# MLP up projection by seven block products instead of eight, with the down projection woven between them

## The chip, the cores and the metric

The kernel runs on one core of one Trainium2 chip. The core has a matrix engine (TensorE, PE in the profile; its weight loads are PEld), three engines for elementwise work (VectorE or DVE, ScalarE or ACT, GpSimd or POOL), a fifth that issues most of the transfers (SyncE or SP), and 16 DMA engines between the main memory and the core's own memory. Matrix products land in PSUM, which has eight banks of 128 x 512 fp32 values. The metric is the device time of one execution in microseconds.

## The reference

A decoder trunk of two layers for 512 tokens of width 1024, in fp32. Each layer has a mixer (pooling and convolution in the first, latent attention in the second), cross-attention into 256 memory tokens, and the gated MLP that this change is about:

```python
def conv_ffn(h, w_up, conv_w, conv_b, w_down):
    a, g = jnp.split(h @ w_up, 2, axis=-1)
    g = causal_dwconv(g, conv_w) + conv_b
    return (jax.nn.silu(g) * a) @ w_down

x = x + conv_ffn(rmsnorm(x, norm_ffn_g[l]), ffn_w_up[l], ffn_conv_w[l], ffn_conv_b[l], ffn_w_down[l])
```

The inner width is 2816, which is 22 tiles of 128. `h @ w_up` has 2 x 22 tiles of output (a and g) and contracts over 1024, 8 tiles of 128; `w_down` contracts over 2816.

## The kernel before

Channels lie on the partitions and the 512 tokens along the free axis, so a tile of activations is 128 x 512. x, the residual stream, stays on chip as 8 such tiles.

Every product is made of three. A value is split into a high part (rounded to the fp32r type, by an ACT copy) and a low part (the value less the high part, by a DVE subtraction), and `mm3` (L156 to L159) adds high x high, high x low and low x high into one PSUM bank. A matmul has a 128 x 128 block of weights as its stationary operand and up to 512 tokens as the moving one. `load_w` (L147) loads 1024 columns of raw weights through SP (`load_raw`, L142, four buffers), casts the high part on ACT (L152) and subtracts the low part on DVE (L153), into three buffers each. These two steps are given a priority that is 40 places higher (`AHEAD`). `linear` (L183) is one output tile: load_w and then 3 matmuls for each k tile.

The order of the instructions on each engine is a planner's: it takes the program's order as priority, and takes a later instruction first where the earlier one isn't ready by its own estimate. Buffers come from pools: `slot` gives one of 58 tiles of 128 x 512 (`SLOTS`), `bank` one of the 8 PSUM banks.

The MLP is `ffn` (L466). Its input is x times the norm's gain, unscaled by the token's rate: the rate is known later (`norm.rate`, `norm.wide`), and is spread to a tile rb that each product is multiplied with on its way out of PSUM (L479, L490). `up(i)` handles a pair of tiles: the gate tile `KF + i`, its convolution over three tokens (ACT L485, DVE L486 and L487), silu (L488), then the tile i, their product (L491), and its split (`split_sb`, L193) into the list prod. After the 9th pair the down projection runs over the first 8 tiles of prod, after the 17th over the next 8, and over the last 6 at the end (`FFN_GROUPS`); each adds its 8 output tiles to x (L514), the last one in layer 0 through `residual` (L288), which also forms the next norm's input. In layer 1 the last group goes through `finale` (L517), which runs 256 tokens at a time. After the third pair of layer 0, `extra` makes the rotary tables (L838), some 20 DVE steps that the second layer's attention uses.

Keys and values of the memory tokens for layer 1 are computed in layer 0's mixer and kept in eight tiles of their own (`keep_whole`, L365) until `split_kv` (L370) at the end of the second layer's attention (L1075).

Of the kernel before, what the change touches and what calls it, by code (L numbers as in the profile page):

```python
# [11 lines left out]
F32 = mybir.dt.float32  # L12
# [7 lines left out]
P = 128  # L20
T = 512
# [29 lines left out]
SLOTS = 58  # L51
# [11 lines left out]
FFN_GROUPS = (8, 8, 6)  # L63

# columns of the packed per-channel constants
# [16 lines left out]
def _split_2pi():  # L82
    """2*pi*512 and 2*pi cut into parts whose products with the counts below are exact in float32."""
# [17 lines left out]
def kernel(ctx: ExitStack, tc: tile.TileContext, a):  # L101
# [7 lines left out]
    pp = ctx.enter_context(tc.tile_pool(name="pp", bufs=8, space=PSUM))  # L109

# [36 lines left out]
    def load_w(src, n):  # L147
        raw = load_raw(src, n)
        hi = wp.tile([P, WCOLS], F32R, tag="wh", name=uid("wh"), bufs=3)
        lo = wp.tile([P, WCOLS], F32R, tag="wl", name=uid("wl"), bufs=3)  # L150
        with tc.high_priority(offset=AHEAD):
            act.copy(hi[:, :n], raw[:, :n])  # L152
            vec.tensor_tensor(lo[:, :n], raw[:, :n], f(hi[:, :n]), ALU.subtract)  # L153
        return hi, lo

    def mm3(ps, ah, al, bh, bl, first, last):  # L156
        pe.matmul(ps, ah, bh, start=first, stop=False)  # L157
        pe.matmul(ps, ah, bl, start=False, stop=False)  # L158
        pe.matmul(ps, al, bh, start=False, stop=last)  # L159

    class Linear:
        """psum[m, t] = sum over k tiles of src[p, k * 128 + m] * xs[k][p, t], a range of k at a time."""

        def __init__(self, src, nk, ps=None):
            self.src, self.nk, self.w = src, nk, {}
            self.ps = bank("lin") if ps is None else ps

        def load(self, k):
            c = k // KD
            if c not in self.w:  # L170
                n = min(KD, self.nk - c * KD) * P
                self.w[c] = load_w(self.src[:, c * KD * P:c * KD * P + n], n)
# [10 lines left out]
    def linear(src, xs):  # L183
        return Linear(src, len(xs)).run(xs, 0, len(xs))
# [15 lines left out]
    def newton_rsqrt(v, n, name):  # L200
        """1/sqrt(v) of a narrow tile."""
# [13 lines left out]
    def col_sums(acc, n=TB):  # L215
        """sums over the partitions of acc, tokens on partitions: [128, n]."""
# [7 lines left out]
    def row_rate(src, n, name):  # L224
        """1/rms of tokens whose features lie along the free axis: [128, n]"""
# [16 lines left out]
    def spread(r, n=TB, name="rb", out=None):  # L242
        """[128, n] with tokens on partitions -> [128, n * 128] with tokens along the free axis."""
# [948 lines left out]
```

## Time and profile before

| | |
|---|---|
| runs | 1388.37 us median of 3 (1388.16 to 1388.73) |
| span of the profiled execution | 1386.6 us |
| what lies around it in the median | 1.8 us |
| first MLP, whole products | about 350 to 668 us |
| second MLP up to its finale | about 1025 to 1341 us |
| loads of weights for up and down in the MLPs | 88 and 48 |

The span is that of one profiled execution, from its first to its last instruction; the runs' median is 1.8 us longer. All times within the kernel below are from that execution, in us from the start of the span. A group's row of the profile gives line, engine, operation, tiles and shapes, a count, and then busy time and mean ns of one. In the timeline a row is start, duration, engine, line and operation. Durations of neighbours overlap on PE, and by somewhat less than 0.1 us on DVE and ACT, so that what an instruction costs its engine is read from the distance between starts.

### The profile page before, as it was taken

The numbers are of one execution on the slowest core, as the hardware profiler recorded it, in microseconds if no ns is written. First come the engines' busy times: TensorE is split into PE (matmuls) and PEld (weight loads), VectorE is DVE, ScalarE is ACT, GpSimd is POOL, SyncE is SP. The second block draws the span as 40 slices with busy tenths as digits, with TensorE's granted clock in tenths as the row PEclk, the third lists the DMA queues.
The fourth block names the chain that finished last, engine by engine and source line by source line (L and its number), as shares of the span: only waits on it lengthen the run. The fifth ranks groups of instructions, "written<-read, shape, count | busy, mean of one in ns | idle before, by whom it ended". The sixth has DMA issues, their size and how long they took to land.

```text
span 1386.6 us, 16884 instructions
## 1 busy us (share of the span) xinstructions
PE 1371.6 (99%) x6532; PEld 1131.2 (82%) x6532; DVE 889.0 (64%) x1535; ACT 599.2 (43%) x976; POOL 6.3 (0%) x17
## 2 busy tenths in 40 slices
PE   8999999999999999999999999999999999999997
PEld 6888978888888888888887776888888888888887
DVE  6999988555685366445669775755566544653565
ACT  6416456443443143223447786644443322332343
POOL 0000000000000000000100000000000000000000
PEclk9999999999999999999999999999999999999999
DMA  9235524113333333333321111321223333233221
GB/s 331 93 106 188 169 91 145 61 56 98 108 97 91 105 93 93 104 91 87 97 83 50 43 46 46 107 76 61 76 91 96 102 92 106 91 93 106 84 84 62
DMA packets 42560, 135.28 MB, mean 98 GB/s; under 512 B 4848, under 2 KB 6512, under 8 KB 42480
## 3 DMA queue, kind: packets, MB, share of 16 engines
q1 hardware_dynamic: 41904, 133.45, 31.0%
q8 instruction: 51, 0.84, 0.2%
q10 hardware_dynamic: 576, 0.76, 0.2%
q14 instruction: 29, 0.24, 0.1%
HBM read 132.09 MB, written 2.10 MB: 97 GB/s over the span
## 4 chain that ended last, share of the span: by engine, by line
PE 90%; DVE 7%; ACT 2%; issue 1%; DMA 0%; SPq 0%; DVEq 0%; ACTq 0%
PE lin L159 24%; PE lin L157 24%; PE lin L158 24%; DVE cv L677 3%; PE s L1016 1%; PE mpv L1053 1%; DVE wl L153 1%; PE t L1041 1%; PE vx L158 1%; PE vx L159 1%; PE fin L157 1%; PE vx L157 1%; PE fin L158 1%; PE fin L159 1%; ACT p L1024 1%
## 5 line engine op out<-in xcount | busy, mean ns | idle before, releaser
L152 ACT CAST wh<-wr 128x1024 fp32r<-128x1024 f32 (+3 forms) x240 | 239.0, 998 | 485.0 <-PE lin L158 338.4
L157 PE MATMUL lin<-hh,wh 128*128 128x512 f32 x976 | 382.4, 392 | 5.9 <-ACT hh L264 5.9
L158 PE MATMUL lin<-hl,wh 128*128 128x512 f32 x976 | 381.1, 391 | 0.0
L159 PE MATMUL lin<-hh,wl 128*128 128x512 f32 x976 | 380.8, 390 | 0.2 <-DVE wl L153 0.2
L153 DVE TENSOR_TENSOR wl<-wr,wh 128x1024 fp32r<-128x1024 f32 (+3 forms) x240 | 276.9, 1155 | 60.4 <-ACT wh L152 58.9
L157 PEld LDWEIGHTS lin<-hh,wh 128*128 128x128 f32 x976 | 183.8, 188 | 43.2 <-ACT hh L264 5.9
L158 PEld LDWEIGHTS lin<-hl,wh 128*128 128x128 f32 x976 | 183.7, 188 | 39.4 <-DVE hl L265 2.1
L159 PEld LDWEIGHTS lin<-hh,wl 128*128 128x128 f32 x976 | 183.7, 188 | 38.7 <-DVE wl L153 0.7
L158 PE MATMUL lin<-fl,wh 128*128 128x512 f32 x304 | 118.4, 389 | 0.0
L159 PE MATMUL lin<-fh,wl 128*128 128x512 f32 x304 | 118.3, 389 | 0.0
L157 PE MATMUL lin<-fh,wh 128*128 128x512 f32 x304 | 118.1, 389 | 0.0
L514 DVE TENSOR_TENSOR x<-x,lin 128x512 f32<-128x512 f32 x32 | 22.0, 688 | 102.8 <-PE lin L159 102.8
L479 DVE TENSOR_TENSOR g<-lin,rb 128x512 f32<-128x512 f32 x44 | 30.4, 690 | 79.2 <-PE lin L159 79.2
L677 DVE SCALAR_TENSOR_TENSOR cv<-a,con,cv 128x509 f32<-128x509 f32 (+25 forms) x115 | 79.5, 728 | 0.1
L490 DVE TENSOR_TENSOR g<-lin,rb 128x512 f32<-128x512 f32 x44 | 30.4, 691 | 71.6 <-PE lin L159 71.4
L158 PEld LDWEIGHTS lin<-fl,wh 128*128 128x128 f32 x304 | 57.1, 188 | 12.1 <-DVE fl L197 0.2
L157 PEld LDWEIGHTS lin<-fh,wh 128*128 128x128 f32 x304 | 57.1, 188 | 11.8
L159 PEld LDWEIGHTS lin<-fh,wl 128*128 128x128 f32 x304 | 57.1, 188 | 11.7
L488 ACT ACTIVATE c<-c 128x512 f32<-128x512 f32 x44 | 27.8, 633 | 82.1 <-DVE c L487 82.1
L289 DVE TENSOR_TENSOR x<-x,lin 128x512 f32<-128x512 f32 x40 | 27.3, 686 | 35.6 <-PE lin L159 35.6
L158 PE MATMUL lin<-ol,wh 128*128 128x512 f32 x128 | 50.1, 391 | 0.0
L159 PE MATMUL lin<-oh,wl 128*128 128x512 f32 x128 | 49.9, 390 | 0.0
(351 smaller groups left out, 2062.4 us busy)
## 6 DMA issues: line engine op xcount, KB each, us to landing
wr<-in_ffn_up SPq DMA_DIRECT2D x88, 512.0 KB, 3.5
wr<-in_ffn_down SPq DMA_DIRECT2D x32, 512.0 KB, 3.5
wr<-in_xa_wk SPq DMA_DIRECT2D x16, 512.0 KB, 3.7
wr<-in_xa_wv SPq DMA_DIRECT2D x16, 512.0 KB, 4.2
wr<-in_xa_wq SPq DMA_DIRECT2D x16, 512.0 KB, 3.6
wr<-in_xa_wo SPq DMA_DIRECT2D x16, 512.0 KB, 3.5
wr<-in_ffn_down SPq DMA_DIRECT2D x16, 384.0 KB, 3.1
wr<-in_pc_in SPq DMA_DIRECT2D x11, 512.0 KB, 6.6
```

The costliest lines, as they stand in the source:

```text
L152: act.copy(hi[:, :n], raw[:, :n])
L153: vec.tensor_tensor(lo[:, :n], raw[:, :n], f(hi[:, :n]), ALU.subtract)
L157: pe.matmul(ps, ah, bh, start=first, stop=False)
L158: pe.matmul(ps, ah, bl, start=False, stop=False)
L159: pe.matmul(ps, al, bh, start=False, stop=last)
L289: vec.tensor_tensor(x[m], x[m], ps, ALU.add)
L479: vec.tensor_tensor(g, gps, rb, ALU.mult)
L488: act.activation(c, c, AF.Silu)
L490: vec.tensor_tensor(g, aps, rb, ALU.mult)
L514: vec.tensor_tensor(x[m], x[m], ps, ALU.add)
L677: vec.scalar_tensor_tensor(cv[i][:, s:], gl[i][:, :T - s], w, cv[i][:, s:], ALU.mult, ALU.add)
L1016: pe.matmul(ps[i], q[:, i * P:(i + 1) * P], k[:, :P * (i + 1)], start=True, stop=True)
```

## The change

The first four pairs of each layer (`PLAIN_PAIRS`) are computed as before, apart from their weights' low parts. For the other 18, the pair's weights are seen as a 2 x 2 block matrix (rows: gate tile and up tile; columns: the two halves of the contraction) and the input as a 2 x 2 block matrix (the two halves of the contraction; the two halves of the tokens). Their product is formed by Winograd's variant of Strassen's scheme: seven block products instead of eight, each over 4 k tiles and 256 tokens, with three matmuls for each k tile as before. Three of the four PSUM groups go on to accumulate after they have been read in between. The operand on the input's side must hold sums of its blocks; `Operands.fill` forms them once a layer, in 32 steps, five after each product of plain pairs 1 to 3, from x scaled by gain and rate. The weights' sums are formed per pair by `Weights.piece`, on DVE.

For the plain pairs from the second on, and for the gate weights of every paired tile, the low part is made by ACT (minus the raw weights, rounded) and an accumulating DMA of POOL that adds the raw weights from main memory.

The down projection runs in groups of four k tiles and one of six. A step of it, three matmuls of 512 columns, follows each of the seven block products. The rotary tables are made after the last of these steps. High and low weights have four buffers instead of three, there are 59 slots, and layer 1's keys and values are stored to main memory and loaded again, instead of in eight tiles of their own.

The core of the diff (comments and docstrings that fall away are left out):

```diff
-SLOTS = 58
+SLOTS = 59
...
-FFN_GROUPS = (8, 8, 6)
+FFN_GROUPS = (4, 4, 4, 4, 6)
+PLAIN_PAIRS = 4
+OPERAND_STEPS = 5
+LEAD = 2
+HALF = T // 2
+KH = KD // 2
...
+    def parts():
+        hi = wp.tile([P, WCOLS], F32R, tag="wh", name=uid("wh"), bufs=4)
+        lo = wp.tile([P, WCOLS], F32R, tag="wl", name=uid("wl"), bufs=4)
+        return hi, lo
+    def low_by_dma(lo, raw, src):
+        act.mul(lo, raw, -1.0)
+        pool.dma_start(lo, src, accum_op=ALU.add)
+    def load_w(src, n, dma=False):
         raw = load_raw(src, n)
-        hi = wp.tile([P, WCOLS], F32R, tag="wh", name=uid("wh"), bufs=3)
-        lo = wp.tile([P, WCOLS], F32R, tag="wl", name=uid("wl"), bufs=3)
+        hi, lo = parts()
         with tc.high_priority(offset=AHEAD):
             act.copy(hi[:, :n], raw[:, :n])
-            vec.tensor_tensor(lo[:, :n], raw[:, :n], f(hi[:, :n]), ALU.subtract)
+            if dma:
+                low_by_dma(lo[:, :n], raw[:, :n], src)
+            else:
+                vec.tensor_tensor(lo[:, :n], raw[:, :n], f(hi[:, :n]), ALU.subtract)
...
     def keep_whole(ps, shape):
-        t = sl.tile(list(shape), F32, tag="kv1", name=uid("kv1"), bufs=8)
+        t = slot("kv1", F32, shape)
         act.copy(t, ps)
+        d = dr.tile(list(shape), F32, tag=uid("kv"), name=uid("kv"))
+        act.dma_start(d, t)
+        return d, shape
...
+    class Operands:
+        def fill(self):
+            low = None
+            for k in range(KH):
+                u = []
+                for kk in (k, k + KH):
+                    t = slot("u")
+                    vec.scalar_tensor_tensor(t, x[kk], col(self.norm.gain, self.norm.base + kk), self.rb,
+                                             ALU.mult, ALU.mult)
+                    u.append(t)
+                    yield
+                b11, b12 = u[0][:, :HALF], u[0][:, HALF:]
+                b21, b22 = u[1][:, :HALF], u[1][:, HALF:]
+                if k % 2 == 0:
+                    low = slot("bh", F32R), slot("bl", F32R)
+                c = slice(k % 2 * HALF, (k % 2 + 1) * HALF)
+                act.copy(low[0][:, c], b11)
+                vec.tensor_tensor(low[1][:, c], b11, f(low[0][:, c]), ALU.subtract)
+                self.v["b11"].append((low[0][:, c], low[1][:, c]))
+                yield
+                a, b = slot("ta"), slot("tb")
+                nt1, nt2 = a[:, :HALF], a[:, HALF:]
+                t3, t4 = b[:, :HALF], b[:, HALF:]
+                vec.tensor_tensor(nt1, b11, b12, ALU.subtract)
+                vec.tensor_tensor(t3, b22, b12, ALU.subtract)
+                yield
+                vec.scalar_tensor_tensor(nt2, t3, -1.0, b11, ALU.mult, ALU.subtract)
+                vec.scalar_tensor_tensor(t4, nt2, -1.0, b21, ALU.mult, ALU.subtract)
+                yield
+                for src, n0, n1 in ((a, "nt1", "nt2"), (u[1], "b21", "b22"), (b, "t3", "t4")):
+                    h, l = split_sb(src, "t")
+                    self.v[n0].append((h[:, :HALF], l[:, :HALF]))
+                    self.v[n1].append((h[:, HALF:], l[:, HALF:]))
+                    yield
+    class Weights:
...
+        def piece(self, n):
+            if n == 0:
+                self.g = load_raw(self.src[0], D)
+                self.r = load_raw(self.src[1], D)
+                hi, lo = parts()
+                act.copy(hi, self.g)
+                low_by_dma(lo, self.g, self.src[0])
+                self.put(("a11", "a12"), hi, lo)
+                return
+            if n == 3:
+                self.split(("a22",), self.r[:, T:])
+                return
+            s = wp.tile([P, WCOLS], F32, tag="ws", name=uid("ws"), bufs=2)
+            if n == 1:
+                self.s2 = s[:, T:]
+                vec.tensor_tensor(s[:, :T], self.r[:, :T], self.r[:, T:], ALU.add)
+                vec.tensor_tensor(s[:, T:], s[:, :T], self.g[:, :T], ALU.add)
+                self.split(("s1", "s2"), s)
+            else:
+                vec.tensor_tensor(s[:, :T], self.r[:, :T], self.g[:, :T], ALU.add)
+                vec.tensor_tensor(s[:, T:], self.s2, self.g[:, T:], ALU.add)
+                self.split(("s3", "s4"), s)
+    SEVEN = (("a11", "b11", 0, 0), ("s1", "nt1", 1, 1), ("s2", "nt2", 1, 0), ("a12", "b21", 0, 2),
+             ("s3", "t3", 2, 0), ("s4", "b22", 2, 1), ("a22", "t4", 3, 0))
...
+        def down():
+            todo = [(n, m) for n in range(len(FFN_GROUPS) - 1) for m in range(KD)]
+            def fetch_w(n, m):
+                raw = load_raw(a["ffn_down"][layer, m][:, starts[n] * P:starts[n + 1] * P], T)
+                return split_sb(raw[:, :T], "dw")
+            nextw = fetch_w(*todo[0])
+            for j, (n, m) in enumerate(todo):
+                hi, lo = nextw
+                ps = bank("down")
+                for k in range(KH):
...
+                    mm3(ps, hi[:, c], lo[:, c], xh, xl, k == 0, k == KH - 1)
+                    if k == 0 and j + 1 < len(todo):
+                        nextw = fetch_w(*todo[j + 1])
+                    if k == KH - 1:
+                        vec.tensor_tensor(x[m], x[m], ps, ALU.add)
+                    yield
...
+        def paired(i):
+            wt = pairs[i]
+            base = (i - PLAIN_PAIRS) * 4
+            ps = [bank("xyz", (P, HALF)) for _ in range(3)]
...
+            for name, other, n, b in SEVEN:
+                need(base + n + LEAD)
+                hi, lo = wt.v[name]
+                for k in range(KH):
+                    s = slice(k * P, (k + 1) * P)
+                    mm3(ps[b], hi[:, s], lo[:, s], *ops.v[other][k], b not in seen and k == 0, k == KH - 1, b in seen)
+                seen.add(b)
+                if name == "a11":
+                    act.copy(q[:, :HALF], ps[0])
+                elif name == "s1":
+                    act.mul(e[:, :HALF], ps[1], -1.0)
+                elif name == "s2":
+                    act.copy(q[:, HALF:], ps[0])
+                elif name == "a12":
+                    vec.tensor_tensor(g[:, :HALF], ps[2], q[:, :HALF], ALU.add)
+                elif name == "s3":
+                    vec.scalar_tensor_tensor(e[:, HALF:], ps[0], -1.0, e[:, :HALF], ALU.mult, ALU.add)
+                elif name == "s4":
+                    vec.tensor_tensor(g[:, HALF:], ps[1], q[:, HALF:], ALU.add)
+                    c = convolved(i, g)
+                else:
+                    vec.scalar_tensor_tensor(c[:, :HALF], ps[0], -1.0, c[:, :HALF], ALU.mult, ALU.mult)
+                    vec.tensor_tensor(c[:, HALF:], c[:, HALF:], e[:, HALF:], ALU.mult)
+                    prod.append(split_sb(c, "f"))
+                next(lower, None)
+        for i in range(PLAIN_PAIRS):
+            if i == PLAIN_PAIRS - 1:
+                need(LEAD)
+            plain(i)
+        fill(100)
+        for i in range(PLAIN_PAIRS, KF):
+            paired(i)
...
+        for _ in lower:
+            pass
...
+        if extra is not None:
+            extra()
+        for m in range(KD):
+            residual(linear(a["ffn_down"][layer, m][:, k0 * P:], prod[k0:]), m, nxt)
```

`need(j)` emits the pieces of weights up to number j, four to a pair, so that each is emitted two pieces ahead of its use. `plain(i)` is the former `up(i)` with its products' weights by `linear(..., True)` from the second pair on and with fill(OPERAND_STEPS) after each product. `convolved` holds the convolution and silu.

More of the change, by code (lines that the diff above doesn't have):

```diff
@@ L471, in ffn @@
         rb = norm.wide()
[L473 to L490 removed]
+        ops = Operands(norm, rb)
@@ L492, in up @@
             prod.append(split_sb(c, "f"))
[L493 to L515 removed]
+        starts = [sum(FFN_GROUPS[:n]) for n in range(len(FFN_GROUPS) + 1)]
```

126 lines of the change are left out of this document (80 added, 46 removed).

## The prediction

> **What bounds the kernel now.** First the page: engine shares, then the waits of PE, then the two MLP stretches.
>
> ```profile
> span 1386.6 us, 16884 instructions
> PE 1371.6 (99%) x6532; PEld 1131.2 (82%) x6532; DVE 889.0 (64%) x1535; ACT 599.2 (43%) x976; POOL 6.3 (0%) x17
> PE 90%; DVE 7%; ACT 2%; issue 1%; DMA 0%; SPq 0%; DVEq 0%; ACTq 0%
> PE lin L157 <- ACT hh L264: 5.9, 1, 5.9
> 350.00:668.00 318.00, 318.00 (x1405) 263.38 (x1404) 178.98 (x226) 107.18 (x130) 0.94 (x2) 1.00 0.32 95
> 1025.00:1341.00 316.00, 316.00 (x1397) 261.65 (x1397) 167.89 (x205) 105.26 (x127) 0.00 (x0) 1.00 0.31 95
> ```
>
> The chain of waits is 90% PE, and PE's longest wait is 5.9 us, once, at the start. The last two rows are stretches of the first and second MLP (length, then busy time of PE, weight loads, DVE, ACT, POOL; granted clock; DMA share; GB/s). PE is busy throughout at clock 1.00, DVE for 56% and 53%, ACT for 34% and 33%. So the MLPs take what their matmuls take. A busy PE says nothing of the rate, since matmuls overlap; the rate is read from the timeline's starts.
>
> ```profile
> 419.78 0.39 PE L158 MATMUL lin<-hl,wh 128*128 128x512 f32 x1
> 431.80 0.39 PE L157 MATMUL lin<-hh,wh 128*128 128x512 f32 x1
> 1351.77 0.28 PE L158 MATMUL fin<-fl,dh 128*128 128x256 f32 x1
> 1357.89 0.28 PE L158 MATMUL fin<-fl,dh 128*128 128x256 f32 x1
> L158 PEld LDWEIGHTS fin<-fl,dh x96: 186/192/192, 1341.7 to 1376.5; 128*128 128x128 f32 x96
> ```
>
> The first pair are the first and last of 54 matmuls with 512 columns: 12.02 / 53 = 226.8 ns apart. The second pair are the first and last of 52 with 256 columns: 6.12 / 51 = 120.0 ns. Each of these matmuls has its own weight load, and 192 ns loads (last row) don't stretch the 120 ns. A matmul thus costs 2 x 120.0 - 226.8 = 13.2 ns beside its columns. That decides what seven products of half width are worth.
>
> **The change, part by part.** *Matmuls.* A pair of tiles (gate i and up i) is now 2 products of 8 k tiles of 3 matmuls: 48 x 226.8 = 10.89 us. The new pair is 7 x 4 x 3 = 84 matmuls of 256 columns: 84 x 120.0 = 10.08 us. The columns fall by an eighth, the gain by 0.81 us is 7%, since 36 more matmuls pay 13.2 ns each. 18 pairs in 2 layers: 36 x 0.81 = 29.0 us. The first 4 pairs of each layer stay, and the down projection keeps its 528 matmuls per layer, so nothing else falls off PE.
>
> The Trainium skill (TensorE: Matmul & The Clock Gate, Back-to-back issue gap) gives N/2.4 plus about 2.5 ns per matmul, 215.8 and 109.2 ns, by which a pair would save 1.19 us and the change 42.7 us (an estimate). The trace disagrees with 226.8 and 120.0 ns, and the measurement decides.
>
> *DVE and ACT beside the pairs.* Back to back, an instruction's price is the distance between starts:
>
> ```profile
> 383.64 1.22 DVE L153 TENSOR_TENSOR wl<-wr,wh 128x1024 fp32r<-128x1024 f32 x1
> 384.77 0.69 DVE L853 SCALAR_TENSOR_TENSOR ang<-rn,ang 128x512 f32<-128x512 f32 x1
> 385.38 0.75 DVE L486 SCALAR_TENSOR_TENSOR c<-g,con,c 128x511 f32<-128x511 f32 x1
> 386.04 0.69 DVE L863 TENSOR_TENSOR ang<-ang,rt 128x512 f32<-128x512 f32 x1
> 386.64 0.75 DVE L487 SCALAR_TENSOR_TENSOR c<-g,con,c 128x510 f32<-128x510 f32 x1
> 1348.68 0.42 DVE L592 TENSOR_TENSOR x<-x,fin 128x256 f32<-128x256 f32 x1
> 1349.01 0.55 DVE L530 TENSOR_TENSOR dl<-wr,dh 128x384 fp32r<-128x384 f32 x1
> 393.11 1.04 ACT L152 CAST wh<-wr 128x1024 fp32r<-128x1024 f32 x1
> 394.04 0.63 ACT L872 ACTIVATE ang<-ang 128x512 f32<-128x512 f32 x1
> 394.57 0.80 ACT L485 ACTIVATE c<-g,con 128x512 f32<-128x512 f32 x1
> ```
>
> DVE: 1.13 us for a 1024-wide low part, 0.61 for 512, 0.66 with a column of constants, 0.33 for 256. ACT: 0.93 for 1024, 0.53 for 512.
> A paired stage's DVE work: four sums of weights 4 x 0.61, low parts 2 x 1.13 + 0.61, five half-width steps 5 x 0.35, two conv steps 2 x 0.66, the product's low part 0.61; with it 7 steps of the down projection, 7/4 of (weights' low part and x sum, 2 x 0.61): 11.1 us. ACT: copies and the negated copy 4 x 0.93 + 0.53, three 256-wide takes 3 x 0.33, c, silu and split 1.8, down weights 7/4 x 0.53: 8.0 us. PE takes 10.08 + 21 x 0.2268 = 14.84 us meanwhile. DVE stands at 75%, ACT at 54%: both still beside PE, at no cost. The cover is 3.7 us a pair; were it gone, each further us costs 36 us in all.
>
> *Filling the operands.* fill() forms the scaled x, its sums and their high and low parts within plain pairs 1 to 3. DVE per k: 2 x 0.66 + 3 x 0.34 + 2 x 0.36 + 3 x 0.61 + a 0.3 us wait for ACT = 5.2, four k: 20.8 us. The three plain pairs' own DVE work without low parts (now by DMA) is 3 x (4 x 0.61 + 2 x 0.66) = 11.3, pair 0's 3.8, the first paired weights (need(LEAD): pieces 1 and 2) 4 x 0.61 + 2 x 1.13 = 4.7. Together 40.6 us. PE's cover from the moment rb exists is 6 products of 5.44 = 32.7 us and the first product of pair 4, 2.1 us: 34.8. Some 2.5 us of the DVE work is needed only later. So DVE is 3.3 us late where PE wants the last sums. PE can be given other work there; that the order on PE isn't the program's is shown here:
>
> ```profile
> 302.13 0.39 PE L157 MATMUL lin<-oh,wh 128*128 128x512 f32 x1
> 302.39 0.50 PE L158 MATMUL lin<-ol,wh 128*128 128x512 f32 x1
> 302.73 0.40 PE L159 MATMUL lin<-oh,wl 128*128 128x512 f32 x1
> 302.97 0.63 PE L157 MATMUL lin<-oh,wh 128*128 128x512 f32 x2
> 303.44 0.40 PE L158 MATMUL lin<-ol,wh 128*128 128x512 f32 x1
> ```
>
> Two L157 stand together where the program has L157, L158, L159: the planner drew a ready matmul forward. Against it stand waits between DVE and ACT that I can't place. Ends: 0 and 8 us a layer (the whole 40.6 with 2.2 us of starts, against 34.8). I take 3, the sum above: 6 us in both layers.
>
> *Low parts by an accumulating DMA.* In the pairs, ACT copies g to hi (0.93), writes -g to lo (0.93), POOL adds the source by DMA. No DMA of POOL and no accumulating one is in this trace. Nearest:
>
> ```profile
> wr<-in_ffn_up SPq DMA_DIRECT2D x88, 512.0 KB, 3.5
> wr<-in_pc_in SPq DMA_DIRECT2D x11, 512.0 KB, 6.6
> wr<-in_pc_out SPq DMA_DIRECT2D x16, 256.0 KB, 2.6
> ```
>
> Below: 3.5 us, a plain load of these bytes. Another 256 KB costs 0.9, so 512 KB read a second time cost 1.8: 5.3, and 0.4 for POOL to issue (its 17 instructions take 6.3 us): 5.7, which I take, as it stands nearest to the load of the same source. Above: twice the 6.6 of the crowded opening, 13.2.
> The window: of 4 weight buffers the first to come free is that of s1 and s2, after the third of seven steps; a step is 12 x 0.120 + 3 x 0.2268 = 2.12 us, so from there to the next pair's a11 are 9.2 us, less 1.9 on ACT: 7.3. A landing in 5.7 costs nothing. POOL has nothing else queued. What waits if it is late is PE's third matmul of a11, with all of PE behind it, unless down steps, 4.76 us a pair, are drawn forward.
>
> The Trainium skill says that an accumulating DMA reads two sources over one ring, so that its rate halves (Collectives: The Full Stack, The bandwidth ceiling), which speaks against the change; with 2.0 us fixed and bytes over 436 GB/s (DMA: Bandwidth & Descriptors, Anatomy of one DMA) that would be 4.4 us, an estimate, and no wait. No run here shows it yet.
>
> In the six plain products that use it, four buffers of 5.44 us leave 16 us: nothing.
>
> *Waits in the pairs.* s2 may go on in bank 0 only when ACT has taken a11 out of it: s1's step of 2.12 us hides 0.33 behind at most one pair of 0.93. The weights of s1 (two sums, cast, low part: 3.3 us) have a12's buffer, 8.5 us before need. SP: two loads a pair and 7/4 for down, as before in bytes; its queue is in order, but 4 raw buffers turn over in a pair and the load takes 3.5. Nothing.
>
> *Slots.* 28 stay with operands, up to 20 with products, 4 with down weights, 6 with q, e, g, c: 58 of 59. A late release holds up ACT and DVE, covered by their idle quarter. I put 0.
>
> *Moved and spilled.* The rotary tables go from pair 2 to before the first layer's last down products:
>
> ```profile
> 374.62 0.42 DVE L844 CAST ang<-pos 128x512 f32<-128x512 int32 x1
> 395.32 0.42 DVE L873 TENSOR_SCALAR ang<-ang 128x512 f32<-128x512 f32 x1
> pos<-in_pos SPq DMA_DIRECT2D x1, 256.0 KB, 4.3
> L153 DVE TENSOR_TENSOR wl<-wr,wh 128x768 fp32r<-128x768 f32 x12 | 11.5, 956 | 0.0
> ```
>
> Some 20 DVE steps of 0.33 to 0.61, 9.4 us, come beside 8 x (2 x 0.61 + 0.66 + 0.87) = 22 us there (x sum, square's sum, low part of x, low part of 768 weights, its 0.956 less the 0.09 that neighbours overlap): 31.4 within 8 x 18 x 0.2268 = 32.7 us of PE. It fits barely; I put 1 us, and 0 to 4. Layer 1's keys and values go to DRAM (8 stores of about 0.33 us on ACT's queue, idle enough) and back by 8 SP loads before their split. They depend on nothing late, so their 2.6 us each are hidden; 0, and 3 if SP holds them behind a full slot.
>
> *Sum.* The profiled span is 1386.6, the median 1388.4, 1.8 more around it, taken as unchanged. -29.0 + 6 + 1 = -22: span 1364.6, time **1366.4**.
>
> **The rivals.** (1) *Filling and tables wholly covered* by drawn-forward work: 1388.4 - 29.0 = 1359.4; for it speaks that PE never waited in these stretches. (2) *DVE or ACT becomes the bound*: 8 us a layer at the filling, 4 at the tables: -29.0 + 20 = 1379; with another 0.2 us a pair, 1386. For it: 75% of DVE in order, slots at 58 of 59. Against: all work of a pair is known a pair ahead. (3) *The other side: the accumulating DMA is late.* Place: a11 of every pair. It decides at a landing of 7.3 us; each us beyond costs 36, so the change breaks even at 7.9. If issue and two full loads add up, 1 + 7.0 = 8.0, 0.7 x 36 = 25: 1391; at 9 us 1428. Against: 5.7, and the down steps to draw forward. (4) *It doesn't do what it says:* half-width matmuls between others take 129.6 ns (10.89 / 84), and the time stays 1388 (with the 7, 1395). Against: 120.0 ns with a weight load each. (5) *A matmul costs its columns alone*: 113.4 ns, -49 + 7: 1346. Against: 13.2 ns measured in this kernel. The Trainium skill's rule above leans this way.
>
> **How the numbers follow.** Forecast 0.42; (1) 0.14; (2) 0.16; (3) 0.20; (4) 0.06; (5) 0.02. The 0.2% that a measurement here can tell from no change are 2.8 us. Faster: 0.42 + 0.14 + 0.14 + 0.02 = 0.72; same: 0.02 of (2), 0.02 of (3), 0.04 of (4) = 0.08; slower: 0.18 + 0.02 = 0.20. The range, 1355 to 1392, leaves out (5) and the later half of (3).
>
> **What would show it.** Half-width matmuls 120 ns apart; DVE near 75% between them; PE waits of about 3 us in each MLP where the first paired products begin; POOL's DMAs landing within 7.3 us of the negated copy; no PE wait on lo or on a bank. Waits of PE on POOL's DMA in each pair would make it wrong, as would spacing near 130 ns or a DVE without idle time.

## The result, and the profile after

The changed kernel takes 1517.22 us (median of 4, 1516.15 to 1519.08) where the kernel before takes 1388.44: a ratio of 1.0929, 95% interval 1.0913 to 1.0944. The forecast of 1366.4 and its range end of 1392 were both too low; what came is the side of the third rival, far beyond its price.

The page of the changed kernel (span, busy time and instructions of each engine, then the chain that ended last, and two rows of DMA issues with KB and median us to landing):

```profile
span 1515.8 us, 20452 instructions
...
PE 1394.7 (92%) x7828; PEld 1196.0 (79%) x7828; DVE 1039.9 (69%) x1919; ACT 751.4 (50%) x1268; POOL 48.8 (3%) x65
...
PE 65%; DMA 20%; DVE 6%; ACT 5%; issue 4%; DVEq 0%; ACTq 0%; POOLq 0%
...
wr<-in_ffn_up SPq DMA_DIRECT2D x88, 512.0 KB, 3.9
wl<-in_ffn_up POOLq DMA_DIRECT2D x48, 512.0 KB, 7.9
```

PE was 90% of the chain and is 65% now. A fifth of it is DMA, of which there was none: POOL's 48 accumulating DMAs, whose median landing is 7.9 us for the bytes that SP's plain loads bring in 3.9. The waits of PE (total us, times, longest) say the same:

```profile
PE xyz L178 <- DMA wl<-in_ffn_up: 60.6, 32, 3.8
PE lin L178 <- DMA wl<-in_ffn_up: 22.2, 4, 7.6
PE xyz L176 <- ACT q L679: 7.9, 2, 3.9
```

The first row is the a11 product of the pairs, 32 of 36 times; the second the plain products, four times; the third the first paired product of each layer. The windows of layer 0's MLP (plain pairs, then pairs) and of layer 1's pairs show what else is lost:

```profile
351.60:412.00 60.40, 41.83 (x160) 32.62 (x160) 37.90 (x66) 27.86 (x42) 3.46 (x4) 0.86 0.35 74
412.00:699.00 287.00, 255.97 (x1683) 236.20 (x1684) 190.03 (x303) 136.00 (x208) 13.84 (x16) 0.95 0.45 116
...
1156.00:1467.00 311.00, 279.97 (x1877) 258.59 (x1877) 202.93 (x325) 146.44 (x224) 14.71 (x17) 0.97 0.45 115
```

Before, PE was busy in all of such stretches at clock 1.00. Now it is idle for 10 to 11% of the paired ones and 31% of the plain one, and the clock is 0.86 to 0.97.

Stages, cut at the first column sum of layer 1's latent attention (the tile's view of kacc, first start in us) and at the last spread of a rate, ahead of the second MLP (the tile's view of rb, last start). Before:

```profile
L219 PE MATMUL st<-ident,kacc x4: 272/272/273, 715.0 to 715.4; 128*128 128x128 f32 x4
```

```profile
L246 PE MATMUL rb<-ident,rny x12: 271/272/273, 349.1 to 1026.0; 128*128 128x128 f32 x12
```

After:

```profile
L238 PE MATMUL st<-ident,kacc x4: 273/273/273, 778.7 to 779.0; 128*128 128x128 f32 x4
```

```profile
L265 PE MATMUL rb<-ident,rny x12: 271/273/323, 351.6 to 1098.6; 128*128 128x128 f32 x12
```

The same marks, in kernels of this study too (told below), give:

| us | start to kacc (has MLP 0) | kacc to rb (latent and cross-attention) | rb to end (MLP 1) |
|---|---|---|---|
| before | 715.0 | 311.0 | 360.6 |
| after | 778.7 | 319.9 | 417.2 |
| e1: no accumulating DMA | 717.6 | 319.4 | 363.9 |
| f2: fetch after the residual | 718.3 | 324.8 | 363.1 |
| g1: the spill alone | 716.4 | 315.0 | 360.5 |
| h2: seven plain pairs | 707.1 | 318.6 | 354.9 |
| h3: h2 and the fetch spread | 707.0 | 315.3 | 353.3 |

The change lost 63.7 us in the first column, 8.9 in the second and 56.6 in the third. The first and third are the MLPs. The second holds no changed product: it holds the fetch of the spilled keys and values.

One pair, from the chain of waits of the changed kernel (start, us, what):

```profile
561.05 0.15 ACT wh L566
...
562.01 0.37 ACT q L683
562.37 0.97 ACT wl L160
...
563.62 9.17 DMA wl<-in_ffn_up
...
572.84 0.39 PE xyz L178
...
573.60 0.21 PE xyz L176
...
576.80 0.19 PE xyz L176
576.99 0.12 PE xyz L177
```

and from its timeline the matmul that waited (in brackets how long, and for what):

```profile
572.84 0.39 PE L178 MATMUL xyz<-bh,wl 128*128 128x256 f32 x1 [2.95 <-DMA wl<-in_ffn_up]
```

This is one of the late ones: the 32 waits are 1.9 us in the mean. The buffer comes free at 561.05, just as the prediction had it, after the third step. ACT casts, takes q out of a bank, writes the negated copy, and POOL issues at 563.62. The matmul could have started at 572.84 - 2.95 = 569.89, so the DMA had 6.27 us, and took 9.17. No down step was drawn ahead of the wait. And this wait costs more than itself: from 573.60 on matmuls of 256 columns stand 0.21 us apart instead of 0.12, until 576.99, at a granted clock of 0.52. In these 3.39 us stand 10 of them and 3 of 512 columns, which take 10 x 0.120 + 3 x 0.227 = 1.88 at full clock: 1.5 us more. Not every wait brings this: behind 11 of the 32 the clock falls within 5 us, behind the other 21 it stays at 1.00.

### The profile page after: what moved, and what is told of

Its sections match the earlier page's. It is cut to its first block, busy times and chain, and to the rows that moved or that the text cites. A ratio compares the mean times of both kernels' runs of the same rounds, so it can differ in the third digit from the quotient of the medians.

```text
span 1515.8 us, 20452 instructions
## 1 busy us (share of the span) xinstructions
PE 1394.7 (92%) x7828; PEld 1196.0 (79%) x7828; DVE 1039.9 (69%) x1919; ACT 751.4 (50%) x1268; POOL 48.8 (3%) x65
## 4 chain that ended last, share of the span: by engine, by line
PE 65%; DMA 20%; DVE 6%; ACT 5%; issue 4%; DVEq 0%; ACTq 0%; POOLq 0%
DMA wl<-in_ffn_up 18%; PE lin L178 10%; PE lin L177 10%; PE lin L176 9%; PE xyz L178 5%; PE xyz L177 4%; PE xyz L176 4%; PE down L178 2%; PE down L176 2%; PE down L177 2%; PE kx L359 2%; ACT wl L160 1%; DMA wr<-in_ffn_up 1%; ACT p L1225 1%; PE vx L178 1%
## 5 line engine op out<-in xcount | busy, mean ns | idle before, releaser
L176 PE MATMUL xyz<-th,wh 128*128 128x256 f32 x864 | 247.7, 287 | 7.9 <-ACT q L679 7.9
L177 PE MATMUL xyz<-tl,wh 128*128 128x256 f32 x864 | 247.1, 286 | 0.0
L178 PE MATMUL xyz<-th,wl 128*128 128x256 f32 x864 | 245.9, 286 | 0.0
L176 PEld LDWEIGHTS xyz<-th,wh 128*128 128x128 f32 x864 | 168.8, 195 | 19.7 <-ACT q L679 8.7
L178 PE MATMUL lin<-hh,wl 128*128 128x512 f32 x400 | 161.8, 405 | 22.4 <-DMA wl<-in_ffn_up 22.2
L177 PEld LDWEIGHTS xyz<-tl,wh 128*128 128x128 f32 x864 | 168.7, 195 | 8.0
L176 PE MATMUL lin<-hh,wh 128*128 128x512 f32 x400 | 163.1, 408 | 10.2 <-ACT hh L283 6.6
L178 PEld LDWEIGHTS xyz<-th,wl 128*128 128x128 f32 x864 | 167.7, 195 | 0.1
L177 PE MATMUL lin<-hl,wh 128*128 128x512 f32 x400 | 161.9, 405 | 3.6 <-DVE hl L284 3.5
L171 DVE TENSOR_TENSOR wl<-wr,wh 128x1024 fp32r<-128x1024 f32 (+3 forms) x124 | 136.9, 1108 | 40.4 <-ACT wh L167 40.4
L557 ACT CAST wh<-ws 128x1024 fp32r<-128x1024 f32 x72 | 75.4, 1048 | 81.2 <-PE xyz L177 77.1
L178 PE MATMUL xyz<-bh,wl 128*128 128x256 f32 x144 | 47.4, 329 | 60.7 <-DMA wl<-in_ffn_up 60.6
```

Of the source, the lines that this page charges most:

```text
L176: pe.matmul(ps, ah, bh, start=first, stop=False, skip_group_check=more)
L177: pe.matmul(ps, ah, bl, start=False, stop=False, skip_group_check=more)
L178: pe.matmul(ps, al, bh, start=False, stop=last, skip_group_check=more)
L557: act.copy(hi[:, :n], raw)
```

## The experiments: the accumulating DMA

**e1** takes the low parts off the DMA everywhere (both hunks), **e2** in the plain products only (the second), **e3** in the pairs only (the first).

```diff
-                hi, lo = parts()
-                act.copy(hi, self.g)
-                low_by_dma(lo, self.g, self.src[0])
-                self.put(("a11", "a12"), hi, lo)
+                self.split(("a11", "a12"), self.g)
...
-            ps = ahead.pop(0) if ahead else linear(a["ffn_up"][layer, KF + i], norm.h, True)
+            ps = ahead.pop(0) if ahead else linear(a["ffn_up"][layer, KF + i], norm.h)
```

> The changed kernel with every low part made by DVE's subtraction again; no accumulating DMA is left, all else stays. Theory A (the accumulating DMA lands too late for its weight buffers, and PE, left idle, gets a lower clock): the waits of PE on the low parts (82.8 us) and the clock loss (0.971 mean) go; DVE has 1.1 us more in each pair and 6.8 us more while it fills the operands, so a few us of wait there; 1370 to 1400 us. Theory B (the block scheme itself is slow here: banks read in between, operands late, in-order DVE): still over 1450 us.

> Low parts by the accumulating DMA only for the gate weights of the 18 pairs of a layer; the six plain products use DVE. Theory A: the waits on the plain products (22.2 us, and the clock near them) go, the 32 waits in the pairs stay: 1475 to 1495 us. Theory B: no change, about 1515.

> Low parts by the accumulating DMA only for the six plain products of a layer; the pairs use DVE. Theory A: the 60.6 us of waits in the pairs and most of the clock loss go, and the plain products go on waiting for buffers that the first pair's weights took early: 1400 to 1430 us. Theory B: over 1450.

Measured: e1 1402.77 us (ratio to before 1.0101, 1.0086 to 1.0116), e2 1488.07 (1.0714, 1.0698 to 1.0730), e3 1432.11 (1.0317, 1.0301 to 1.0332). e2 is in its band; e1 and e3 lie 2 to 3 us above theirs, far below the rival's. The DMA in the plain products thus costs 1517.22 - 1488.07 = 29.2 us, in the pairs 1517.22 - 1432.11 = 85.1; the sum, 114.3, takes 1517.2 to 1402.9, and e1 is at 1402.8. The two are separate and account for 114 of the 129 us. The 85.1 are 24.5 more than the 60.6 us of waits; the low clock is of that size, with 5% of 287 us and 3% of 311, together some 24.

**e4** keeps the DMA but halves the buffers: eight of 512 columns, so that a11 and a12 each have one of their own, and what they overwrite comes free sooner.

```diff
-        hi = wp.tile([P, WCOLS], F32R, tag="wh", name=uid("wh"), bufs=4)
-        lo = wp.tile([P, WCOLS], F32R, tag="wl", name=uid("wl"), bufs=4)
+        hi = wp.tile([P, T], F32R, tag="wh", name=uid("wh"), bufs=8)
+        lo = wp.tile([P, T], F32R, tag="wl", name=uid("wl"), bufs=8)
```

> Same memory for weights, but in 8 buffers of 512 columns instead of 4 of 1024, each weight tile as two halves with a cast and a low part (or an accumulating DMA of 256 KB) each. A pair uses seven of the eight, so that a11's half is free for the next pair about a pair (15 us) before its use. If the buffer window is what makes the DMA late: waits on the low parts in the pairs all but go, 1390 to 1430 us. If the accumulating DMA is slow whatever the lead (its queue, or what it takes from the other loads): over 1480 us.

Measured: 1421.26 us (1.0235, 1.0216 to 1.0253). From its page, its windows and its waits:

```profile
wl<-in_ffn_up POOLq DMA_DIRECT2D x96, 256.0 KB, 4.3
```

```profile
353.00:412.00 59.00, 45.15 (x186) 36.07 (x187) 42.61 (x76) 32.15 (x58) 7.76 (x9) 0.86 0.47 99
412.00:699.00 287.00, 286.25 (x1950) 264.09 (x1949) 226.46 (x396) 166.40 (x309) 31.45 (x39) 1.00 0.51 128
```

In the pairs PE is busy for 286.25 of 287 us at clock 1.00, with the same bytes through the same queue. So it wasn't POOL's or the DMA's throughput: it was one landing against one buffer's window. e4 changes both sides of that comparison, since half the bytes land sooner (4.3 us) and half a buffer comes free sooner, and doesn't say which of them was needed. What e4 keeps is the loss ahead of 412 us, and there only 5.6 of PE's 13.8 idle us are waits for the DMA; 6.7 are one wait for ACT's copy out of a bank in the first pair.

In the plain products the prediction saw 16 us of slack. POOL's and ACT's timelines of the changed kernel:

```profile
354.14 0.87 POOL L161 DMA_DIRECT2D wl<-in_ffn_up  x1 [5.82 <-ACT wl L160]
360.84 0.86 POOL L161 DMA_DIRECT2D wl<-in_ffn_up  x1 [5.84 <-ACT wl L160]
376.69 0.86 POOL L161 DMA_DIRECT2D wl<-in_ffn_up  x1 [14.98 <-ACT wl L160]
```

```profile
358.02 1.04 ACT L566 CAST wh<-wr 128x1024 fp32r<-128x1024 f32 x1
...
362.99 1.06 ACT L557 CAST wh<-ws 128x1024 fp32r<-128x1024 f32 x1 [1.57 <-PE lin L177]
...
368.43 1.06 ACT L557 CAST wh<-ws 128x1024 fp32r<-128x1024 f32 x1 [0.48 <-PE lin L177]
...
373.87 1.05 ACT L167 CAST wh<-wr 128x1024 fp32r<-128x1024 f32 x1 [2.26 <-PE lin L177]
```

The first and the third of these DMAs belong to plain products, the second to the first pair's gate weights. Between the two plain ones ACT cast three buffers for the first pair's weights (L566, L557 twice), which the program asks for ahead of the last plain pair. They hold three of the four buffers, and the plain products go on with one: its cast waited for PE, its DMA was issued at 376.69, and PE waited for it:

```profile
383.33 0.80 PE L178 MATMUL lin<-hh,wl 128*128 128x512 f32 x1 [7.63 <-DMA wl<-in_ffn_up]
383.92 0.63 PE L176 MATMUL lin<-hh,wh 128*128 128x512 f32 x1
...
389.04 0.43 PE L176 MATMUL lin<-hh,wh 128*128 128x512 f32 x1
```

This is read from the trace; no run kept the DMA and moved that request.

## The experiments: what e1 still loses

By the forecast, which put the DMA at nothing, e1 would be at 1366; it is 14.3 us above before. Its pairs do what was forecast. Timeline, the same DVE instruction of ten pairs in a row (first and last), and windows:

```profile
440.30 0.42 DVE L686 TENSOR_TENSOR g<-xyz,q 128x256 f32<-128x256 f32 x1 [1.22 <-PE xyz L178]
...
574.39 0.42 DVE L686 TENSOR_TENSOR g<-xyz,q 128x256 f32<-128x256 f32 x1 [0.19 <-PE xyz L178]
```

```profile
371.00:401.00 30.00, 21.47 (x84) 16.44 (x84) 27.94 (x49) 13.61 (x23) 0.00 (x0) 0.86 0.19 62
...
440.00:660.00 220.00, 220.00 (x1551) 206.12 (x1550) 182.85 (x286) 110.58 (x176) 0.00 (x0) 1.00 0.33 102
```

Nine pairs in 134.09 us are 14.90 each, with PE busy throughout at clock 1.00 and DVE at 83%. The loss is the passage from plain to paired products: from 371 to 401 us PE is idle for 8.5 us and runs the rest at 0.86, some 13 us in all, while DVE is busy for 27.94 of 30.

**f1** asks for the first pair's weights only after the plain pairs, so that buffers come free (first diff); **f3** has six plain pairs instead of four with three operand steps at a time (second); **f4** has both and f2's edit (below).

```diff
-            if i == PLAIN_PAIRS - 1:
-                need(LEAD)
```

```diff
-PLAIN_PAIRS = 4
-OPERAND_STEPS = 5
+PLAIN_PAIRS = 6
+OPERAND_STEPS = 3
```

> As e1_low_by_dve, but the first paired tile's weights are no longer emitted ahead of the fourth plain pair (the need(LEAD) in the loop goes; paired() asks for them itself). In e1 PE waits and lower clock cost about 13 us a layer between plain and paired products. If three of the four weight buffers taken early by the pair's pieces cause it: 8 to 20 us less than e1's 1402.8, 1383 to 1395. If DVE's backlog from filling the operands causes it (it is busy 93% there): no change within 3 us.

> As e1_low_by_dve, but six plain pairs with three filling steps after each product instead of four with five. If DVE's backlog from filling is what makes the first paired products late: the wait of 13 us a layer goes, two pairs a layer lose their 0.81 us: 1383 to 1392 us. If the early weights are the cause: about e1, 1400 to 1407.

> The three edits of f1, f2 and f3 together on e1_low_by_dve. If the losses of e1 are these places and nothing else, the matmul saving is left: 1388.4 less 16 times 0.81 times 2 (26) and a few us of waits, 1363 to 1372 us. If another part of the change costs time: over 1380.

Measured: f1 1406.45 us (1.0132, 1.0115 to 1.0149), f3 1400.94 (1.0092, 1.0077 to 1.0107), f4 1400.18 (1.0086, 1.0071 to 1.0101). f1 is 3.7 us over e1. Its waits between 345 and 440 us:

```profile
PE xyz L176 <- ACT bh L522: 5.6, 1, 5.6
PE xyz L176 <- ACT q L676: 5.3, 1, 5.3
```

The waits only moved, from the plain products to the first pair's operands (bh). Early buffers were not what bounded e1; something behind both was. f3 and f4 gave little: f3 lies where early weights as the cause would have put it, which f1 speaks against, and f4 misses its 1363 to 1372 by 28 us. By their times alone it stayed open whether that is VectorE's backlog. The chain of waits of f1 speaks for it: from 379.63 to 400.79 us it holds VectorE's steps and 0.7 us of issue (time in which an engine waits for nothing that the profile shows), and then PE goes on:

```profile
379.63 0.60 DVE tl L216
...
400.18 0.61 DVE dwl L216
...
400.84 0.80 PE down L178
```

**g2** moves the operand sums of f3 to the idle GpSimd.

```diff
-                vec.tensor_tensor(nt1, b11, b12, ALU.subtract)
-                vec.tensor_tensor(t3, b22, b12, ALU.subtract)
+                pool.tensor_tensor(nt1, b11, b12, ALU.subtract)
+                pool.tensor_tensor(t3, b22, b12, ALU.subtract)
...
-                vec.scalar_tensor_tensor(nt2, t3, -1.0, b11, ALU.mult, ALU.subtract)
-                vec.scalar_tensor_tensor(t4, nt2, -1.0, b21, ALU.mult, ALU.subtract)
+                pool.tensor_tensor(nt2, b12, b22, ALU.subtract)
+                pool.tensor_tensor(nt2, nt2, b11, ALU.subtract)
+                pool.tensor_tensor(t4, t3, b11, ALU.add)
+                pool.tensor_tensor(t4, t4, b21, ALU.subtract)
```

> f3 (low parts by VectorE, six plain pairs) with the four sums of each operand step on the idle GpSimd instead of VectorE: 16 instructions of 0.42 us, 6.7 us a layer, leave VectorE (GpSimd takes 24 small ones, since it forms two of the sums in two steps). Theory (the passage from plain to paired products is lost to VectorE's backlog of filling): f3 loses some 10 us a layer there, idle and low clock together, and 3 to 6 of them go: 1389 to 1395 us. Rival (it is the order on ScalarE's queue, or GpSimd's sums come later than VectorE's): 1399 to 1406 us.

Measured: 1415.39 us (1.0194, 1.0178 to 1.0209), worse than both theories allowed. GpSimd's groups:

```profile
L530 POOL TENSOR_TENSOR tb<-u,u 128x256 f32<-128x256 f32 x8 | 14.8, 1844 | 2.2 <-DVE u L513 2.2
...
L533 POOL TENSOR_TENSOR ta<-ta,u 128x256 f32<-128x256 f32 x8 | 6.7, 840 | 0.0
```

A sum takes 0.84 to 1.84 us there in the mean of its group, against 0.42 on VectorE, and there are six instead of four; the chain of sums became the late one. The run tells nothing about the backlog.

**h1** takes work off VectorE without giving it to anyone: the low parts of the operands are left out (first diff; b11 likewise). **h2** takes nothing off, but gives PE more work beside it: seven plain pairs, down products drawn from the fifth on, and the first pair's weights asked for a piece at a time (second diff).

```diff
-                    h, l = split_sb(src, "t")
-                    self.v[n0].append((h[:, :HALF], l[:, :HALF]))
+                    h = slot("th", F32R)
+                    act.copy(h, src)
+                    self.v[n0].append((h[:, :HALF], h[:, :HALF]))
```

```diff
-PLAIN_PAIRS = 4
-OPERAND_STEPS = 5
+PLAIN_PAIRS = 7
+OPERAND_STEPS = 3
...
+        def draw(i, n):
+            for _ in range(n if i >= FFN_GROUPS[0] else 0):
+                next(lower)
...
+            draw(i, 3)
+            if i == PLAIN_PAIRS - 1:
+                need(0)
...
+            draw(i, 4)
+            if i == PLAIN_PAIRS - 1:
+                need(1)
```

> e1 (low parts of the weights by VectorE) without the low parts of the operand sums: VectorE's 16 subtractions of a layer's filling are left out (12 of 0.69 us and 4 of 0.42 us, 9.9 us a layer) and the products take the high parts a second time, so PE has the same matmuls. Theory (the passage is lost to VectorE's backlog: in e1 VectorE has some 57 us of work in 45): nearly all of it goes, 8 to 11 us a layer with the low clock behind the waits: 1381 to 1387 us. Rival (ScalarE's order or the weights' landing is the bound, as GpSimd's run left possible): 1398 to 1403 us.

> e1 with seven plain pairs, three operand steps at a time, the down products drawn from plain pair 4 on, and the first two weight pieces of the paired stage asked for one product each ahead. No work is taken off VectorE; PE gets more beside it: six plain pairs of 10.9 us and 21 steps of down products of 0.68 us, some 80 us, against VectorE's some 75. Theory (backlog): the waits at the passage go, three of 18 paired tiles' gain of 0.81 us a layer with them: 1402.8 less 2 x (13 - 2.4) = 1380 to 1386 us. Rival (not the backlog): 1398 to 1404 us.

Measured: h1 1391.55 us (1.0021, 1.0012 to 1.0030): 11.2 us under e1, so 5.6 a layer for 9.9 us of VectorE work. That is between the two bands: the backlog is a part of the loss, some 13 us a layer, and not relieved one for one. In h1 PE still waits 3.2 us at the first pair for ACT's copy out of a bank, which stands on ACT behind casts of operands. h2 1380.52 us (0.9942, 0.9925 to 0.9958), in its band's lower end: 22.3 us under e1, with VectorE's filling as it was. Of PE's waits between 345 and 470 us two remain, 0.8 and 0.5 us. So the passage looks like a matter of how much PE work stands beside VectorE's; h2 changes the requests for weights too, and the next run keeps those.

**h4** against h3 (which is h2 with another fetch, below) finds the point where it turns: six plain pairs, four operand steps at a time.

> h3 with six plain pairs and four operand steps at a time: one more tile of each layer is paired (1.6 us in all gained), and VectorE has some 68 us of work beside PE's some 64. Theory (backlog): 2 to 6 us a layer come back as waits at the passage, so 2 to 10 us above h3. Rival (the plan with seven has room to spare): 1 to 2 us below h3.

Measured: 1390.59 us (1.0015, 1.0006 to 1.0024), 12.7 above h3's 1377.93, more than expected. Windows of h3 and then of h4, over the same 20 us:

```profile
372.00:392.00 20.00, 18.68 (x82) 14.84 (x81) 18.13 (x33) 9.30 (x15) 0.00 (x0) 1.00 0.12 39
```

```profile
372.00:392.00 20.00, 17.02 (x76) 13.75 (x74) 19.19 (x34) 10.01 (x16) 0.00 (x0) 1.00 0.12 42
392.00:432.00 40.00, 37.67 (x177) 31.62 (x178) 30.39 (x47) 16.73 (x26) 0.00 (x0) 0.91 0.29 93
```

With four steps at a time VectorE is busy for 19.19 of 20 us, PE waits 5.3 us for the first down weights, and the clock falls to 0.91 behind it; in h3 the waits at that place are 1.4 us and the clock stays at 1.00. Pairs and steps alone thus bring the loss back.

## The experiments: the spill

**g1** is the kernel before with the spill of layer 1's keys and values alone. **f2** (e1 with the fetch and splits moved behind the residual products) and **g3** (f3 with the fetch through the raw weight buffers instead of slots) move it; **h3** (h2) fetches and splits one tile after each residual product, through the raw weight buffers.

f2:

```diff
-        kv = split_kept(kv)
         for m in range(KD):
...
             residual(ps, m, nxt)
-        return kv
+        return split_kept(kv)
```

g3, and h3 too:

```diff
     def fetch(kept):
         d, shape = kept
-        t = slot("kv1", F32, shape)
+        raw = wp.tile([P, WCOLS], F32, tag="wr", name=uid("wr"), bufs=4)
+        t = raw[:, :T]
```

h3 alone, where `keys` is split_kept made into a generator:

```diff
-        kv = split_kept(kv)
         for m in range(KD):
...
             residual(ps, m, nxt)
+            next(keys, None)
```

> The kernel before with one part of the change alone: layer 1's keys and values are written to DRAM and fetched back into slots of the pool ahead of the latent attention's residual products; the MLP is the old one. Theory (the spill costs 8 to 10 us, read from the stage between the latent sum and the second MLP in all runs so far): 1396 to 1398 us, the loss in that stage. Rival (that stage is longer only because of what the new MLP hands over, such as buffers or the order of the loads): 1388 to 1390 us.

> As e1_low_by_dve, but layer 1's keys and values are fetched and split after the attention's output products instead of ahead of them. From the kernel before to e1 the stretch between the second layer's latent products and its MLP grew from 310.7 to 319.1 us. If the fetch and the 16 splits in front of the residual steps cost these 8.4 us: 1394 to 1398 us. If it is something else of the change (buffers, slots): 1402 to 1404.

> f3 with the spilled keys and values fetched into the raw weight buffers instead of into slots. Theory (the fetches wait for free slots and hold SyncE's queue, so the weights behind them come late): the stage between the latent sum and the second MLP falls from 318.6 us to 311 to 313, in all 1393 to 1396 us. Rival (the fetched bytes and their landing are the cost, wherever they land): 1400 to 1402 us.

> h2 with the spilled keys and values fetched and split one a residual product, through the raw weight buffers, where the other kernels do all eight ahead of the first. Theory (the fetch's cost is the eight late splits, which hold up the residual's splits, or in g3 the four buffers taken at once): the stage between the latent sum and the second MLP falls from some 319 us to 311 to 313, so 6 to 8 us under h2. Rival (spreading them moves the lateness to the attention that follows): within 2 us of h2.

Measured: g1 1393.58 us (1.0037, 1.0025 to 1.0050), 5.0 over before where 8 to 10 were expected. In the profiled execution it is 4.0 in the second column of the table and 1.4 ahead of it. f2 1408.45 (1.0145, 1.0130 to 1.0161), g3 1405.16 (1.0122, 1.0107 to 1.0137; f3: 1400.94): neither remedy helped, and both came out above either of their bands. Waits of PE in f2, in g3, and in g1:

```profile
PE sx L176 <- ACT qh L208: 9.9, 1, 9.9
```

```profile
PE lin L176 <- ACT wh L167: 7.1, 1, 7.1
```

```profile
PE lin L159 <- DVE hl L266: 2.1, 5, 0.9
```

In g1 the loads come late, and so do the splits; ScalarE and VectorE do them where they should form the residual's high and low parts (hl). The waits for hl are 2.1 of the 5.0 us. The splits of the values (duration min/median/max in ns, first and last start in us) in the tile's view of kv, before and then in g1, there with the loads:

```profile
L196 ACT CAST vh<-kv x8: 613/616/619, 207.3 to 879.7; 128x512 fp32r<-128x512 f32 x8
```

```profile
L197 ACT CAST vh<-kv x8: 613/620/623, 209.0 to 897.1; 128x512 fp32r<-128x512 f32 x8
...
L376 SPq DMA_DIRECT2D kv<-kv x8: 327/383/425, 839.2 to 893.4; - x8
```

The last split is 17.4 us later than before, because the last load is issued at 893.4. What held it is not its own slot. SP's waits between 870 and 900 us, when the last six loads are issued, are all waits of weight loads (L145) for a raw buffer, and a load of kv goes out right behind one of them:

```profile
SPq L145 <- DVE wl L154: 52.5, 7, 34.2
```

In f2 eight splits in a row stand ahead of the attention's own (qh), and PE waits for those; in g3 eight loads take the four raw buffers at once, and PE waits for weights. h3: 1377.93 us (0.9923, 0.9909 to 0.9938), 2.6 under h2, between its two bands; the second column falls from 318.6 to 315.3, half of what was expected. 4.3 us against before stay there; their cause isn't settled.

**g4** put f1's, f3's, g2's and g3's edits together; g2's and g3's results were not known then.

> All three remedies with low parts by VectorE: six plain pairs, the sums on GpSimd, the fetch through the raw weight buffers, and the first paired weights asked for only after the plain products. If the costs add as in the runs so far: 1400.9 less 6 to 12 for the filling, less 5 to 8 for the fetch: 1381 to 1390 us, with 1388.4 before. Rival (the remedies share one bound and do not add): 1392 to 1396 us.

Measured: 1411.17 us (1.0162, 1.0147 to 1.0177), above both of its bands. The late sums of g2 and the weights' wait of g3 are both in it.

**h3** is the version that beats both kernels: 10.5 us under the kernel before, with seven-product pairs for 15 of 22 tiles a layer and no accumulating DMA.

## Why the prediction was wrong, step by step

- **The matmul's price: right.** 84 matmuls at 120.0 ns and 21 at 226.8 gave 14.84 us a pair; e1 shows 14.90. Rivals (4) and (5) are out. By the Trainium skill's gap of a single matmul (TensorE: Matmul & The Clock Gate, Back-to-back issue gap) a pair would be 13.70, an estimate, which e1 contradicts too.
- **DVE and ACT beside the pairs: right.** 75% and 54% were forecast with the DMA. e1 gives VectorE one more low part, 1.13 us of 14.84, 7.6%: 82.6% by the count, 182.85 / 220 = 83.1% measured. Neither held PE there, so rival (2) is out for the pairs.
- **The accumulating DMA: the step that failed.** "5.7, which I take, as it stands nearest to the load of the same source" measured 7.9 in the median and 5.9 to 9.3. The window, "9.2 us, less 1.9 on ACT: 7.3", is 6.27 in the pair shown: 8.84 us from the free buffer to the matmul, less 2.57 until POOL issues, since ACT also takes q out of a bank (0.36) and 0.28 pass between ACT and POOL. Rival (3) had the place, the mechanism and both numbers' ends (3.5 to 13.2), and I gave it 0.20. Its price was too low as well: at 7.9 us it says 0.6 x 36 = 22, and the pairs lost 85.1, since the window is a microsecond shorter and some of the waits bring the low clock. "Unless down steps are drawn forward" did not happen.
- **"In the six plain products ... 16 us: nothing": wrong, 29.2 us.** Four buffers were counted as if all were the plain products' own, though the prediction's count for the filling has the request for the first pair's weights in it, which takes three of them.
- **Filling: the count was right, its cover was not.** 40.6 us of DVE work against 34.8 of PE work holds with the low parts on the DMA. With them on VectorE (7 of 1.13 us) the same count gives 48.5, of which 2.5 are needed later, against 34.8: 11.2 us late, where e1 loses some 13 a layer. That is the place of rival (2), and it speaks against rival (1) at the filling. The 3 us forecast for the change itself were never tested apart, since the DMA's waits lie over them; at the first paired product PE waited 3.9 us a layer, for ACT's copy of q.
- **Rotary tables: about nothing, 1 us forecast.** In e1, DVE is busy for all of 680 to 700 us and PE doesn't wait there.
- **The spill: 0 forecast, 3 as the other end; 5.0 alone.** "They depend on nothing late" left out the queue: in g1 the loads stand on SP's queue behind weight loads that wait for raw buffers. The other end, "if SP holds them behind a full slot", had the queue right and the place wrong. The eighth is issued at 893.4 us, and its split falls among the residual's.
- **The sum.** The DMA's 114.3 and the 14.3 that e1 still loses are 128.6 of the 128.8 us. h3 shows the forecast's gain in part: 15 pairs a layer at 0.81 us would be 24.3 us; 10.5 are left after 4.3 in the attention stage and some 9 more, spread over the start, remaining waits and a less dense plan, which no run separates.

## What to carry to other kernels

An asynchronous step that takes the place of work on an engine is priced by its slowest landing against the shortest time that its buffer leaves, and a miss of a microsecond or two in a tight loop is paid in nearly every round, in some rounds with the clock on top; if the price is unknown and the break-even is 2 us off, that term decides the chance of the whole forecast. Count the buffers of a pool over all that draw from it at that moment, the next stage's requests too (read from a trace here, not tested alone). Where one engine is loaded at a passage between two stages, lengthen the work beside it before moving its work elsewhere: h2 gained 22 us with more matmuls beside the filling, g2 lost 14 by moving sums.

## What the runs showed of the hardware

- An accumulating DMA from GpSimd's queue of 512 KB landed in 7.9 us, of 256 KB in 4.3: the second 256 KB cost 3.6, taken between two kernels (the changed one and e4). SP's plain loads took 3.9 and 2.7 in the changed kernel, 1.2 for the second. These transfers add, land in the fp32r type and go through another queue; no run has them apart. The Trainium skill tells of the add in a reduce-scatter that it reads two sources over one ring, which halves the rate (Collectives: The Full Stack, The bandwidth ceiling). Here that has the right sign, and the estimate of 4.4 us made from it is too low by 3.5. The tile's view of wl has the spread (us to landing):

```profile
DMA to landing us min/median/max: 5.9/7.9/9.3
```

- The granted clock can halve after a short wait of PE: behind 2.95 us, 256-column matmuls stood 0.21 us apart for 3.4 us; behind 7.63 us, 512-column ones 0.43 apart from 383.92 to 389.04. Of the 32 waits for the DMA in the pairs, the 14 of up to 1.23 us brought no fall, the 18 of 1.82 to 3.81 us brought 11; the shortest with a fall was 1.82, the longest without one 2.94. So between these two the length of a wait doesn't settle it. The Trainium skill (TensorE: Matmul & The Clock Gate, What's actually happening) has half clock after an idle window of about 3.4 us and full clock after as long a busy one; the trace agrees in the length of the ramp after the 2.95 us wait, and shows falls after waits shorter than that window.
- An elementwise sum on GpSimd took two to four times VectorE's 0.42 us. The Trainium skill gives about twice (GPSIMD Engine Reference, Engine selection); the trace has group means from 0.84 to 1.84, with the caution that its times on GpSimd are rough.
